# Mixture-of-experts routing of a hybrid decoder trunk: squares summed row by row on TensorE, and the routing stage's steps in another order

## Chip, cores and metric

One core of one Trainium2 chip. The metric is the device time of one execution in microseconds (us), of which the median of several runs is given. A profile is one execution recorded by the hardware profiler; its "span" runs from the first to the last recorded instruction, and times inside it count from the span's start.

## What is computed

Two layers on 512 tokens of width 1024. The first is a gated short convolution with a dense SwiGLU channel mixer, the second is multi-head latent attention with a routed channel mixer: of 8 experts each token uses the best 2. The change lies between the attention's output projection and the first expert. Cut to that part, the reference is:

```python
x = x + mla_mixer(h, ...)                       # ends in  o @ w_o
h = rmsnorm(x, norm_ffn[1])
probs = softmax(h @ router)
vals, idx = lax.top_k(probs, 2)
gates = one_hot(idx) weighted by vals / sum(vals)
for e in range(8):
    out = out + gates[:, e:e+1] * swiglu(h, w_gate[e], w_up[e], w_down[e])
x = x + out
```

All products are wanted at fp32 quality. The kernel splits each operand into a high and a low part (xh and xl, w_hi and w_lo) and adds up two or three products.

## The kernel before, in words

The residual stream lies transposed in `xT`: 8 rows ("fo") of 128 features by 512 tokens. From the attention on, the program's order on each engine is the order in which the code is written out; nothing is reordered by a planner. An engine's queue is worked off in order, so an instruction that waits holds up all that stands behind it on that engine.

The stage of the change runs in these steps.

- Output projection, a loop over 8 rows (line 877). TensorE makes six matmuls of 512 columns (`out_mm`, lines 688 to 690) and, from the third row on, two for the router's logits of the row two before (`logits`, lines 872 and 873; the second needs `xlr`, the low half of that row). VectorE adds the row to `xT` (line 882), makes the low half of the row before (line 888) and one eighth of the first expert weight chunk's low half (line 120). ScalarE makes the high half (885), the squares (891) and one eighth of the chunk's high half (117). GpSimd adds the squares to `acc` (893).
- Token rows. The experts gather whole tokens, so `xT` is transposed back, in 8 blocks of 128 tokens by 512 features. `rows_mm(i)` (line 909) makes four transposes into one PSUM bank. `rows_ev(i)` makes a scaled high half on ScalarE (line 914) and then, out of the same bank and that high half, the low half on VectorE (line 915). `base(i)` (line 921) copies the same bank unscaled to `hs`, mostly on ScalarE, and SyncE sends `hs` to the output.
- Norm and ranking. The sum of squares over features comes from matmuls of one column with `acc` as stationary operand (942). The norm `r3` is a power on GpSimd (line 248, from line 1137). Ranking the 8 logits of a token takes VectorE lines 1139 to 1149 and ends in `sel`. Matmuls with `tri` and `ones_b` count positions into `pc` (1151 to 1153), VectorE turns them into `pos` (1159) and one-hot columns `oh1` (1168). `keep_warm(n)` issues n matmuls whose result is not used (949).
- Picks. Expert 0's tokens are taken by matmuls with `oh1`: `pick(f, 0)` from the high and `pick(f, 1)` from the low half of the token rows, four matmuls each (1189), for 8 rows f. Each picked bank is scaled to `xe` by ScalarE (1200) and VectorE (1201). Then the first expert's matmuls start (1033).
- Expert 0's one-hot list for the gather of its token numbers is made on GpSimd (`select`, 968); GpSimd also issues the four transfers of the token rows to DRAM (1181).

PSUM has 8 banks. Two hold `plt` (later `idle`, which also serves `rows_mm(6)`) and `misc`; six go round in turn among the projection's rows, the transposed rows and the picked rows. Before the change these are, in order: rows_mm 0 to 5 and 7, then picks 0 to 7; each takes the bank of the sixth allocation before it.

Of the kernel before, what the change touches and what calls it, by code (L numbers as in the profile page):

```python
# [11 lines left out]
F32 = mybir.dt.float32  # L12
F32R = mybir.dt.float32r
BF16 = mybir.dt.bfloat16
I32 = mybir.dt.int32
AF = mybir.ActivationFunctionType
# [139 lines left out]
def hybrid_trunk_kernel(ctx, tc, xT_in, pos_in, vecs_in, rope_g, invf_in, ident_in, cst_in, info_in, dslot_in,  # L156
# [713 lines left out]
    def logits(fo):  # L870
        xh, xl = split.pop(fo)
        mm(plt[0:2 * NE, :], rhl[:, fo, :], xh, start=fo == 0, stop=False)
        mm(plt[0:NE, :], rhl[:, fo, 0:NE], xl, start=False, stop=fo == NB - 1)

    ws.pool, ws.ahead, ws.limit, ws.manual = wmoe, 2, len(chunks), True
    pieces = ws.split([256] * 8, True)
    for fo in range(NB):
        ps = ops.tile([P, T], F32, name="ps", tag="ps")
        pairs[3].out_mm(ps, fo)
        if fo >= 2:  # L880
            logits(fo - 2)
        tt(xT[:, fo, :], ps, xT[:, fo, :], ALU.add)
        xh = ot.tile([P, T], F32R, name="xhr", bufs=3)
        xl = ot.tile([P, T], F32R, name="xlr", bufs=3)
        nc.scalar.copy(xh, xT[:, fo, :])
        if fo > 0:
            pxh, pxl = split[fo - 1]
            tt(pxl, xT[:, fo - 1, :], pxh.bitcast(F32), ALU.subtract)
        split[fo] = xh, xl
        sq = acc if fo == 0 else ot.tile([P, T], F32, name="sq", tag="sq")  # L890
        act(sq, xT[:, fo, :], AF.Square)
        if 0 < fo < NB - 1:
            nc.gpsimd.tensor_tensor(acc, acc, sq, ALU.add)
        if fo < NB - 1:
            next(pieces)
    tt(xl, xT[:, NB - 1, :], xh.bitcast(F32), ALU.subtract)
# [7 lines left out]
    def rows_mm(i, ps=None):  # L904
        hf, tb = divmod(i, TB)
        ps = ps or ops.tile([P, T], F32, name="ps", tag="ps")
        hps.append(ps)
        for j in range(4):
            nc.tensor.transpose(ps[:, j * P:(j + 1) * P], xT[:, hf * 4 + j, tb * P:(tb + 1) * P], ident)
# [7 lines left out]
    def base(i, copy):  # L917

        hf, tb = divmod(i, TB)
        hs = bp.tile([P, T], F32, name="hs")  # L920
        copy(hs, hps[i])
        nc.sync.dma_start(out[tb * P:(tb + 1) * P, hf * T:(hf + 1) * T], hs)

    for i in range(4):
        rows_mm(i)
    logits(NB - 2)
    logits(NB - 1)
    rows_mm(4)
    for i in range(2):
        base(i, nc.scalar.copy)  # L930
    lgt = ot.tile([2 * NE, T], F32, name="lgt", bufs=1)
    nc.scalar.copy(lgt, plt[0:2 * NE, :])
    tt(acc, acc, sq, ALU.add)
    for i in range(2, 4):
        base(i, nc.vector.tensor_copy)
    list(pieces)
    for tb in range(TB):
        nc.tensor.transpose(misc[:, tb * 2 * NE:(tb + 1) * 2 * NE], lgt[:, tb * P:(tb + 1) * P],
                            ident[0:2 * NE, 0:2 * NE])
    for tb in range(TB):  # L940
        t_s = slice(tb * P, (tb + 1) * P)
        mm(pss[:, tb:tb + 1], acc[:, t_s], ones[:, 0:1], start=tb == 0, stop=tb == TB - 1)
    rows_mm(5)
    idle = lps.tile([P, T], F32, name="plt")

    def keep_warm(n):

        for _ in range(n):
            mm(idle, ones_b, ones_b[:, None, :].to_broadcast([P, TB, P]), start=True, stop=True)

    keep_warm(6)
    ws.split_hi()
    for i in range(4, 6):
        base(i, nc.scalar.copy)
    octx.close()


# [168 lines left out]
    def ot1(shape, name, dt=F32):  # L1126
        return ot.tile(shape, dt, name=name, tag=name)
# [19 lines left out]
    rank = cpool.tile(sh3, F32, name="rank")  # L1147
    nc.vector.tensor_reduce(rank, cmp, axis=AX.X, op=ALU.add)
    ts(sel_b, rank, 2.0, None, op0=ALU.is_lt)

    mm(pc, tri, sel, start=True, stop=False)
    for tb in range(TB):
        mm(pc[:, tb + 1:, :], ones_b, sel[:, tb:tb + 1, :].to_broadcast([P, TB - tb, NE]), start=False, stop=tb == TB - 1)
    keep_warm(6)
    rows_mm(6, idle)
    mx = ot1([P, TB], "mx4")
    nc.vector.tensor_reduce(mx, lg, axis=AX.X, op=ALU.max)
    pos = cpool.tile(sh3, F32, name="pos")
    stt(pos, pc[:, 0:TB, :], 1.0, sel_b, op0=ALU.add, op1=ALU.mult)
    cnt = cpool.tile([P, NE], F32, name="cnt")  # L1160
    nc.vector.tensor_copy(cnt, pc[:, TB, :])
    ex = [Expert(ws.chunk, e % 2, CAPS[e]) for e in range(NE)]


# [1 line left out]
    oh1 = ot1([P, TB, c0], "oh1", F32R)  # L1166
    for tb in range(TB):
        ts(oh1[:, tb], iota[:, 0:c0], pos[:, tb, 0:1], None, op0=ALU.is_equal)
    ex[0].select(pos[:, :, 0:1])
    xe2 = ep.tile([P, NB, 2, 2, CAP], F32R, name="xe", bufs=1)  # L1170
    xb2 = ep.tile([P, NB, 2, CAP], BF16, name="xb", bufs=1)
    ex[0].hold()
    for i in range(8):
        rows_ev(i)
        if i == 0:
            rows_mm(7)
    for i in (6, 7):
        base(i, nc.scalar.copy)
    for part, op in enumerate((ALU.bypass, ALU.add)):
        for hf in range(2):  # L1180
            nc.gpsimd.dma_start(hrow.rearrange("(t p) d -> p t d", p=P)[:, :, hf * T:(hf + 1) * T],
                                tr[part][hf].bitcast(F32), accum_op=op)
    picked = {}

    def pick(f, part):
        if part == 0:
            picked[f] = ops.tile([P, T], F32, name="ps", tag="ps")[:, 0:c0]
        for tb in range(TB):
            mm(picked[f], tr[part][f // 4][:, tb, (f % 4) * P:(f % 4 + 1) * P], oh1[:, tb],
               start=part == 0 and tb == 0, stop=part == 1 and tb == TB - 1)  # L1190

    pick(0, 0)
    for f in range(NB):
        if f < NB - 1:
            pick(f + 1, 0)
        pick(f, 1)
        pv = picked[f]
        g = col(V_FFN1 + f)
        xe = ex[0].xe
        act(xe[:, f, 0, :], pv, AF.Copy, scale=g)  # L1200
        stt(xe[:, f, 1, :], pv, g, xe[:, f, 0, :].bitcast(F32), op0=ALU.mult, op1=ALU.subtract)
        if f % 4 == 3:
            f4 = slice(f - 3, f + 1)
            nc.scalar.copy(ex[0].xb[:, f4, :], xe[:, f4, 0, :].bitcast(F32))
# [114 lines left out]
    for e in range(NE):  # L1319
        x, nxt, prv = ex[e], ex[e + 1] if e + 1 < NE else None, ex[e - 1] if e else None  # L1320
        for c in range(24):
            storing = prv and prv.nh == 2 and 0 < c < 5
            loading = nxt and NF <= c < NF + LOADS
            if storing:
                prv.store_mm(c - 1)
            if loading:
                nxt.load_mm(c - NF)
            if c < NF:
                x.hidden_mm(c)
                if c > 2 and c % 2:  # L1330
                    x.hidden_split(c // 2 - 1)
                if c and c % 2 == 0:
                    x.hidden_gate()
                x.hidden_add(c)
            else:
                x.down_mm(c - NF)
                if c == NF:
                    x.hidden_gate()
                if c == NF + 1:
                    x.hidden_split(NF // 2 - 1)  # L1340
                if c % 4 == 3:
                    (x.down_add if nxt else last_store)((c - NF) // 4)
            if storing:
                prv.store_ev(c - 1)
            if loading:
                nxt.load_ev(c - NF)
            if prv and c == (2 if prv.nh == 2 else 0):
                prv.store(0)

            if prv and c == 13 and prv.nh == 2:  # L1350
                prv.store(1)
            if not nxt and c == 11:
                last_base()
            if ws.n_split <= last_k:
                ws.split_hi()
            if ws.n_lo <= last_k:
                ws.split_lo()
            while ws.n_raw <= min(ws.n_split - 1 + len(ws.ring), last_k):
                list(ws.load())
            if e == 1 and c == 10:  # L1360
                extra_rows()
            if e == 0:
                if c == 0:
                    rank_experts()
                if c == 1:
                    x.find(0)
                    ranked(posn, pos)
                    ranked_weights()
                if c in (2, 3):
                    nxt.select(posn[:, :, 0:1], (2 * c - 4, 2 * c - 3))  # L1370
                if c == 3:
                    ranked_gates()
                if c == 4:
                    xctx.close()
                    xtctx.close()
                    late.append(right(ctx, "late"))
                    ws.grow(late[0], 2)
            if e + 2 < NE and NF <= c < NF + TB:
                ex[e + 2].select(posn[:, :, e + 2 - NS:e + 3 - NS], (c - NF,))
            if nxt and c == 6:  # L1380
                nxt.find(e + 1)
                nxt.gather()
# [205 lines left out]
```

## Time and profile before

| | us |
|---|---|
| median of 3 runs | 1408.69 (1407.62 to 1410.09) |
| the profiled execution | 1409.13 |
| its span | 1407.4 |
| stage of the change, projection of the first row to the first expert matmul | 748.3 to 786.3 |

TensorE is busy for 98% of the span, VectorE for 71%, ScalarE for 58%, GpSimd for 20%. In the profile PE is TensorE's matmuls and PEld its weight loads, which overlap; DVE is VectorE, ACT ScalarE, POOL GpSimd, SP SyncE. A row of a timeline gives start, duration, engine, line, operation, output and input, the number of instructions merged into it, and in brackets the idle time before it with what ended that.

### The profile page before, as it was taken

Reading aid. Unit: us, or ns where it says so; the run is one execution under the profiler, and the core shown is the slowest. Engines: PE = TensorE matmul, PEld = TensorE weight load, DVE = VectorE, ACT = ScalarE, POOL = GpSimd, SP = SyncE. Lnnn points to the kernel's source line nnn. Section 1 sums busy time; section 2 is a strip of 40 time slices with the busy share of each in tenths; the row PEclk is TensorE's granted clock in tenths of the full one; section 3 lists DMA queues with packets and bytes.
Section 4 is the critical chain, followed back from the end, with each engine's and each line's share of the span. In section 5 each row is a group of like instructions: output and inputs, shape, how many; then the busy total and the mean of one; then the engine's idle time right before and its main releaser. Section 6 shows DMA issues by size and latency. Waiting matters only on the chain. (4 is left out here: it accounts for less than half of the span.)

```text
span 1407.4 us, 23788 instructions
## 1 busy us (share of the span) xinstructions
PE 1375.7 (98%) x9543; PEld 1197.0 (85%) x9544; DVE 993.4 (71%) x1263; ACT 815.2 (58%) x1210; POOL 286.1 (20%) x206
## 2 busy tenths in 40 slices
PE   9999999999999999999998999999999999999996
PEld 6888888888888887878876899999999999979794
DVE  7754565442344444587788897898889899999895
ACT  6222332222222233677645787878888788988893
POOL 0000000000000000143302432342614343453231
PEclk9999999999999999999999999999999999999998
DMA  6332222322223222101203999998999999999993
GB/s 223 112 115 91 90 90 94 116 90 90 90 93 117 91 90 92 64 31 63 82 10 149 310 358 373 308 331 300 347 329 334 360 341 368 321 400 370 384 364 104
DMA packets 49390, 284.40 MB, mean 202 GB/s; under 512 B 9320, under 2 KB 11112, under 8 KB 17272
## 3 DMA queue, kind: packets, MB, share of 16 engines
q1 hardware_dynamic: 41688, 269.82, 52.7%
q0 software_dynamic: 7584, 12.98, 3.9%
q8 instruction: 77, 1.26, 0.4%
q14 instruction: 41, 0.34, 0.1%
HBM read 271.39 MB, written 11.37 MB: 201 GB/s over the span
## 5 line engine op out<-in xcount | busy, mean ns | idle before, releaser
L97 DVE TENSOR_TENSOR w_lo<-w_raw,w_hi 128x2048 bf16<-128x2048 f32 (+1 forms) x239 | 556.9, 2330 | 53.9 <-ACT w_hi L88 53.6
L88 ACT CAST w_hi<-w_raw 128x2048 fp32r<-128x2048 f32 x239 | 456.6, 1910 | 221.5 <-PE ps L256 158.8
L1033 PE MATMUL gu<-xe,w_hi 128*128 128x304 f32 (+6 forms) x2048 | 288.9, 293 | 0.0
L1033 PEld LDWEIGHTS gu<-xe,w_hi 128*128 128x128 f32 x2048 | 264.1, 189 | 0.4
L255 PE MATMUL ps<-xh,w_hi 128*128 128x512 f32 x592 | 232.4, 393 | 2.2 <-ACT xh L290 1.3
L256 PE MATMUL ps<-xl,w_hi 128*128 128x512 f32 x592 | 231.0, 390 | 0.3 <-DVE xl L291 0.3
L257 PE MATMUL ps<-xh,w_lo 128*128 128x512 f32 x592 | 231.1, 390 | 0.0
L1047 POOL TENSOR_TENSOR sg<-sg,p 128x304 f32<-128x304 f32 (+6 forms) x64 | 88.0, 1374 | 304.6 <-ACT sg L1046 300.6
L1033 PE MATMUL gu<-xb,w_lo 128*128 128x152 bf16 (+6 forms) x2048 | 143.4, 223 | 3.9 <-DVE w_lo L97 3.9
L255 PEld LDWEIGHTS ps<-xh,w_hi 128*128 128x128 f32 x592 | 111.5, 188 | 26.8 <-ACT xh L290 1.8
L256 PEld LDWEIGHTS ps<-xl,w_hi 128*128 128x128 f32 x592 | 111.6, 188 | 24.1 <-DVE xl L291 0.8
L1033 PEld LDWEIGHTS <-w_lo 128*128 128x128 bf16 x2048 | 120.6, 98 | 12.8 <-DVE w_lo L97 5.8
L257 PEld LDWEIGHTS ps<-xh,w_lo 128*128 128x128 f32 x592 | 111.5, 188 | 23.3
L248 POOL TENSOR_TENSOR rs<-m,mhalf 128x4 f32<-128x4 f32 x3 | 3.1, 1020 | 590.8 <-DVE m L505 555.9
L1077 PE MATMUL gu<-ae,w_hi 128*128 128x304 f32 (+3 forms) x640 | 97.4, 302 | 0.0
L257 PE MATMUL ps<-ah,w_lo 128*128 128x512 f32 x240 | 94.7, 394 | 0.0
L255 PE MATMUL ps<-ah,w_hi 128*128 128x512 f32 x240 | 94.6, 394 | 0.0
L256 PE MATMUL ps<-al,w_hi 128*128 128x512 f32 x240 | 94.6, 394 | 0.0
L1077 PEld LDWEIGHTS gu<-ae,w_hi 128*128 128x128 f32 x640 | 87.1, 189 | 0.0
L1041 DVE TENSOR_TENSOR p<-gu,p 128x304 f32<-128x304 f32 (+6 forms) x128 | 55.7, 435 | 23.7 <-ACT p L1040 22.5
L1040 ACT COPY p<-gu 128x304 f32<-128x304 f32 (+6 forms) x128 | 49.3, 385 | 38.7 <-PE gu L1033 38.0
L968 POOL TENSOR_SCALAR oh<-rest,posn 128x152 bf16<-128x152 f32 (+6 forms) x28 | 60.1, 2159 | 1.3 <-DVE posn L1258 1.3
(334 smaller groups left out, 1878.7 us busy)
## 6 DMA issues: line engine op xcount, KB each, us to landing
w_raw<-w_moe SPq DMA_DIRECT2D x192, 1024.0 KB, 8.5
w_raw<-w_a SPq DMA_DIRECT2D x50, 1024.0 KB, 4.8
w_raw<-w_hp SPq DMA_DIRECT2D x4, 1088.0 KB, 5.1
w_raw<-w_o SPq DMA_DIRECT2D x4, 1024.0 KB, 4.7
xT<-xT_in SPq DMA_DIRECT2D x8, 256.0 KB, 5.0
out<-hs SPq DMA_DIRECT2D x8, 256.0 KB, 4.1
hrow<-xh POOLq DMA_DIRECT2D x2, 1024.0 KB, 5.9
hrow<-xl POOLq DMA_DIRECT2D x2, 1024.0 KB, 23.6
```

Of the source, the lines that this page charges most:

```text
L88: self.nc.scalar.copy(hi[:, :w], self.raw[k][:, :w])
L97: self.nc.vector.tensor_tensor(lo[:, :w], self.raw.pop(k)[:, :w], self.hi[k][:, :w].bitcast(F32), ALU.subtract)
L248: nc.gpsimd.tensor_tensor(out_t, m, h, ALU.pow)
L255: mm(ps, wh, xh[:, kc, :], start=kc == 0, stop=False)
L256: mm(ps, wh, xl[:, kc, :], start=False, stop=False)
L257: mm(ps, wl, xh[:, kc, :], start=False, stop=kc == n - 1)
L968: nc.gpsimd.tensor_scalar(s.oh[:, tb, 0:s.cap], iota[:, 0:s.cap], p[:, tb], None, op0=ALU.is_equal)
L1033: mm(s.ps[:, i, 0:n], w[:, b:b + P], x[:, kc], start=w is hi and kc == 0, stop=w is lo and kc == NB - 1)
L1040: nc.scalar.copy(p2, s.ps[:, :, s.cap:2 * s.cap])
L1041: tt(p2, s.ps[:, :, 0:s.cap], p2, ALU.add)
L1047: nc.gpsimd.tensor_tensor(s.sg, s.sg, s.p2[:, :, 1], ALU.mult)
L1077: mm(s.dp[q // 2][:, q % 2, 0:n], w[:, b:b + P], x[:, 4 * kq + j], start=w is hi and kq + j == 0, stop=w is lo and kq + j == 6)
```

## The change

It makes these edits.

1. Squares. GpSimd no longer adds them up. `square_sums(fo)` makes four matmuls of one column per row, with the row's squares as stationary operand, accumulated over all rows in `pss`. Rows 0 to 5 are summed inside the loop, two rows late; rows 6 and 7 behind their logits. VectorE's last addition of squares and the four matmuls on `acc` go.
2. Order on TensorE after the loop: logits and squares of rows 6 and 7, then the transposes of the logits, then `rows_mm(4)`, 6 warming matmuls; `rows_mm(5)` moves among the picks.
3. `base(2)` and `base(3)` go from VectorE to ScalarE. `base(4)` and `base(5)` move from ahead of the norm to behind `rows_ev` of the same block.
4. The high half of the second weight chunk (`ws.split_hi`, 128x2048 on ScalarE) moves from ahead of the token rows to behind `base(7)`, which is ahead of the picks' evictions.
5. `rows_ev(0)` stands ahead of the counting, `rows_ev(1)` to `rows_ev(4)` behind `oh1`, `rows_ev(5)` to `rows_ev(7)` each followed by its `base`. The second warming has 4 matmuls, not 6. `cnt` and `mx` move behind.
6. `select` of expert 0 moves on GpSimd from ahead of the four transfers to between the second and the third, and `find(0)` from the expert's chunk 1 to chunk 2.
7. The picks of high halves run two rows ahead of the low ones, not one.

```diff
+    sqs = {}
+
+    def square_sums(fo):
+        sq = sqs.pop(fo)
+        for tb in range(TB):
+            mm(pss[:, tb:tb + 1], sq[:, tb * P:(tb + 1) * P], ones[:, 0:1],
+               start=fo == 0 and tb == 0, stop=fo == NB - 1 and tb == TB - 1)
+
     for fo in range(NB):
         ps = ops.tile([P, T], F32, name="ps", tag="ps")
         pairs[3].out_mm(ps, fo)
         if fo >= 2:
+            square_sums(fo - 2)
             logits(fo - 2)
...
-        sq = acc if fo == 0 else ot.tile([P, T], F32, name="sq", tag="sq")
-        act(sq, xT[:, fo, :], AF.Square)
-        if 0 < fo < NB - 1:
-            nc.gpsimd.tensor_tensor(acc, acc, sq, ALU.add)
+        sqs[fo] = acc if fo % 3 == 2 else ot.tile([P, T], F32, name="sq", tag="sq")
+        act(sqs[fo], xT[:, fo, :], AF.Square)
...
-    logits(NB - 2)
-    logits(NB - 1)
-    rows_mm(4)
+    for fo in (NB - 2, NB - 1):
+        logits(fo)
+        square_sums(fo)
...
-    tt(acc, acc, sq, ALU.add)
-    for i in range(2, 4):
-        base(i, nc.vector.tensor_copy)
...
-    for tb in range(TB):
-        t_s = slice(tb * P, (tb + 1) * P)
-        mm(pss[:, tb:tb + 1], acc[:, t_s], ones[:, 0:1], start=tb == 0, stop=tb == TB - 1)
-    rows_mm(5)
+    for i in range(2, 4):
+        base(i, nc.scalar.copy)
+    rows_mm(4)
...
     keep_warm(6)
-    ws.split_hi()
-    for i in range(4, 6):
-        base(i, nc.scalar.copy)
...
     ts(sel_b, rank, 2.0, None, op0=ALU.is_lt)
+    rows_ev(0)
...
-    keep_warm(6)
-    rows_mm(6, idle)
+    keep_warm(4)
...
-    ex[0].select(pos[:, :, 0:1])
...
-    for i in range(8):
+    for i in range(1, 5):
         rows_ev(i)
-        if i == 0:
-            rows_mm(7)
-    for i in (6, 7):
-        base(i, nc.scalar.copy)
...
     pick(0, 0)
+    rows_mm(5)
+    base(4, nc.scalar.copy)
+    pick(1, 0)
+    rows_mm(6, idle)
+    rows_mm(7)
+    for i in range(5, 8):
+        rows_ev(i)
+        base(i, nc.scalar.copy)
+    ws.split_hi()
...
+    for part, op in enumerate((ALU.bypass, ALU.add)):
+        for hf in range(2):
+            nc.gpsimd.dma_start(hrow..., tr[part][hf].bitcast(F32), accum_op=op)
+        if part == 0:
+            ex[0].select(pos[:, :, 0:1])
     for f in range(NB):
-        if f < NB - 1:
-            pick(f + 1, 0)
+        if f < NB - 2:
+            pick(f + 2, 0)
         pick(f, 1)
...
+                if c == 2:
+                    x.find(0)
                 if c == 1:
-                    x.find(0)
```

## Rows read from the trace of the kernel before

**Rows 1.** The page: span, then busy time, share of the span, instructions.
```profile
span 1407.4 us, 23788 instructions
...
PE 1375.7 (98%) x9543; PEld 1197.0 (85%) x9544; DVE 993.4 (71%) x1263; ACT 815.2 (58%) x1210; POOL 286.1 (20%) x206
```

**Rows 2.** Busy time by stretch: projection loop, ranking, counting, the experts.
```profile
core 0: us, PE busy (x) PEld busy (x) DVE busy (x) ACT busy (x) POOL busy (x), PEclk, DMA share, GB/s
752.50:766.50 14.00, 11.19 (x46) 6.84 (x45) 14.00 (x18) 8.94 (x20) 7.30 (x6) 1.00 0.54 229
...
770.90:775.50 4.60, 4.58 (x22) 2.88 (x23) 3.05 (x10) 4.60 (x7) 1.02 (x1) 0.65 0.86 315
775.50:778.60 3.10, 2.81 (x21) 1.63 (x19) 2.70 (x9) 2.55 (x6) 2.40 (x4) 0.96 1.05 332
...
900.00:1000.00 100.00, 99.79 (x989) 97.16 (x989) 85.57 (x92) 80.22 (x100) 37.56 (x21) 1.00 0.92 322
```

**Rows 3.** Timeline of PE: projection loop and what follows it.
```profile
751.83 0.39 PE L688 MATMUL ps<-xh,w_hi 128*128 128x512 f32 x1
...
753.67 0.40 PE L688 MATMUL ps<-xh,w_hi 128*128 128x512 f32 x1
...
766.54 1.91 PE L909 MATMUL ps<-ident,xT 128*128 128x128 f32 x16
768.21 0.47 PE L872 MATMUL plt<-xhr,rhl 128*16 128x512 f32 x1
...
770.92 0.42 PE L938 MATMUL misc<-ident,lgt 16*128 16x16 f32 x4 [0.39 <-ACT lgt L932]
...
775.53 0.24 PE L1151 MATMUL misc<-sel,tri 128*128 128x40 bf16 x1
```

**Rows 4.** Timeline of PEld: square sums, transposes and warming at half clock, picks.
```profile
771.27 0.97 PEld L942 LDWEIGHTS misc<-ones,acc 128*128 128x128 f32 x8
772.08 0.71 PEld L909 LDWEIGHTS ps<-ident,xT 128*128 128x128 f32 x4
772.76 0.36 PEld L949 LDWEIGHTS <-ones_b 128*128 128x128 bf16 x2
...
783.13 0.52 PEld L1189 LDWEIGHTS ps<-oh,xh 128*128 128x128 f32 x4 [0.26 <-ACT hs L921]
...
786.25 2.40 PEld L1033 LDWEIGHTS gu<-xe,w_hi 128*128 128x128 f32 x16
```

**Rows 5.** Timeline of DVE: low half beside POOL and alone, positions, token rows.
```profile
754.18 1.66 DVE L888 TENSOR_TENSOR xlr<-xT,xhr 128x512 fp32r<-128x512 f32 x1
...
757.79 0.68 DVE L888 TENSOR_TENSOR xlr<-xT,xhr 128x512 fp32r<-128x512 f32 x1
...
775.90 0.19 DVE L1159 SCALAR_TENSOR_TENSOR pos<-misc,sel 128x32 f32<-128x32 f32 x1 [1.57 <-PE misc L1153]
...
777.11 4.03 DVE L915 SCALAR_TENSOR_TENSOR xl<-ps,r,xh 128x512 fp32r<-128x512 f32 x6
781.06 0.74 DVE L915 SCALAR_TENSOR_TENSOR xl<-plt,r,xh 128x512 fp32r<-128x512 f32 x1
781.72 0.74 DVE L915 SCALAR_TENSOR_TENSOR xl<-ps,r,xh 128x512 fp32r<-128x512 f32 x1
```

**Rows 6.** Timeline of ACT: weight chunk, token rows, their copies, the picks' evictions.
```profile
771.08 1.89 ACT L88 CAST w_hi<-w_raw 128x2048 fp32r<-128x2048 f32 x1
772.88 1.05 ACT L921 COPY hs<-ps 128x512 f32<-128x512 f32 x2
...
778.60 0.69 ACT L914 ACTIVATE xh<-ps,r 128x512 fp32r<-128x512 f32 x1 [0.26 <-PE ps L909]
781.83 0.59 ACT L921 COPY hs<-plt 128x512 f32<-128x512 f32 x1 [2.55 <-DVE xl L915]
782.49 0.59 ACT L921 COPY hs<-ps 128x512 f32<-128x512 f32 x1
782.98 1.23 ACT L1200 ACTIVATE xe<-ps,vec 128x152 fp32r<-128x152 f32 x4
```

More of the change, by code (lines that the diff above doesn't have):

```diff
@@ L1153, in hybrid_trunk_kernel @@
         mm(pc[:, tb + 1:, :], ones_b, sel[:, tb:tb + 1, :].to_broadcast([P, TB - tb, NE]), start=False, stop=tb == TB - 1)
-    keep_warm(6)
-    rows_mm(6, idle)
-    mx = ot1([P, TB], "mx4")
-    nc.vector.tensor_reduce(mx, lg, axis=AX.X, op=ALU.max)
+    keep_warm(4)
     pos = cpool.tile(sh3, F32, name="pos")
     stt(pos, pc[:, 0:TB, :], 1.0, sel_b, op0=ALU.add, op1=ALU.mult)
-    cnt = cpool.tile([P, NE], F32, name="cnt")
-    nc.vector.tensor_copy(cnt, pc[:, TB, :])
     ex = [Expert(ws.chunk, e % 2, CAPS[e]) for e in range(NE)]
@@ L1168, in hybrid_trunk_kernel @@
         ts(oh1[:, tb], iota[:, 0:c0], pos[:, tb, 0:1], None, op0=ALU.is_equal)
-    ex[0].select(pos[:, :, 0:1])
-    xe2 = ep.tile([P, NB, 2, 2, CAP], F32R, name="xe", bufs=1)
-    xb2 = ep.tile([P, NB, 2, CAP], BF16, name="xb", bufs=1)
-    ex[0].hold()
-    for i in range(8):
-        rows_ev(i)
-        if i == 0:
-            rows_mm(7)
-    for i in (6, 7):
-        base(i, nc.scalar.copy)
[L1179 to L1182, printed above, removed]
+    for i in range(1, 5):
+        rows_ev(i)
     picked = {}
@@ L1192, in hybrid_trunk_kernel @@
     pick(0, 0)
+    rows_mm(5)
[7 more added lines that the diff above has]
+    ws.split_hi()
+    cnt = cpool.tile([P, NE], F32, name="cnt")
+    nc.vector.tensor_copy(cnt, pc[:, TB, :])
+    mx = ot1([P, TB], "mx4")
+    nc.vector.tensor_reduce(mx, lg, axis=AX.X, op=ALU.max)
+    xe2 = ep.tile([P, NB, 2, 2, CAP], F32R, name="xe", bufs=1)
+    xb2 = ep.tile([P, NB, 2, CAP], BF16, name="xb", bufs=1)
+    ex[0].hold()
+    for part, op in enumerate((ALU.bypass, ALU.add)):
+        for hf in range(2):
+            nc.gpsimd.dma_start(hrow.rearrange("(t p) d -> p t d", p=P)[:, :, hf * T:(hf + 1) * T],
+                                tr[part][hf].bitcast(F32), accum_op=op)
+        if part == 0:
+            ex[0].select(pos[:, :, 0:1])
     for f in range(NB):
-        if f < NB - 1:
-            pick(f + 1, 0)
+        if f < NB - 2:
+            pick(f + 2, 0)
         pick(f, 1)
```

## Prediction

> **What bounds the kernel now.** I read the page first: TensorE is busy for 98% of the span, every other engine for 71% or less [rows 1]. A share over the whole span doesn't say what a stage is worth, so the next view was busy time by stretch. In the experts, from 786 us to the end nearly, PE is busy for 99.79 of 100 us at full clock [rows 2]. Nothing there can make up for a late start: what the stage before hands over late is late at the end. So the number to forecast is the start of the first expert matmul, 786.25 us by its weight load [rows 4].
>
> The stage before it has three parts, and their limits differ. In the projection loop VectorE is busy for 14.00 of 14.00 us while TensorE has 11.19 [rows 2]: TensorE waits for `xlr`. The reader sees why in the timeline of VectorE: the same subtraction takes 0.68 us alone and 1.66 us while GpSimd adds squares [rows 5]. In ranking and counting the granted clock of TensorE is 0.65 on average, that is a mix of 2.4 and 1.2 GHz [rows 2]. In the last part VectorE makes the eight low halves one behind the other, 777.11 to 782.46 [rows 5], and TensorE's picks follow, each as soon as a PSUM bank and the rows are there; the only wait in it was 0.26 us for a copy to `hs` [rows 4].
>
> **Part 1, the loop.** One row with logits is eight matmuls, 751.83 to 753.67: 1.84 us [rows 3]. Six such rows make 11.04 us; from 751.83 to the first token-row transpose at 766.54 it took 14.71 [rows 3]. The 3.67 us between are the wait for VectorE. With GpSimd's additions gone, VectorE has per row two operations of 0.68 us [rows 5] and a smaller one, below a row of TensorE, so I count that wait as gone. What is late next is TensorE itself: `square_sums` is eight passes per row. The same eight passes on `acc` ran from 771.27 to 772.08, 0.81 us [rows 4]; by the price of a transpose, 1.67 us for 16 from 766.54 to 768.21 [rows 3], they would be 0.84. A pass has one column only, and its weight load sets the pace, so they don't hide beside the matmuls. The loop becomes 6 x (1.84 + 0.81) = 15.9 us: it ends at 767.73, 1.2 us later than before. Bounds: if half of each sum hides behind 512-column matmuls, 1.2 us earlier than before; if the loads run at 0.97 us per row (the whole span of the eight loads [rows 4]), 2.2 us later. I take 0.81, the operation's own row.
>
> **Part 2, from the loop to the positions.** TensorE then has 16 transposes (1.67), two logits pairs (0.46 each, a quarter of 1.84), two square sums (0.81 each): 767.73 + 4.21 = 771.94. The logits' copy on ScalarE fits beside the last sum. The four small transposes take 0.35 (770.92 to 771.27 [rows 3, 4]), `rows_mm(4)` 0.5 to 0.7, six warming matmuls at half clock 2.77 (772.76 to 775.53 [rows 3, 4]): the counting starts at about 775.5 to 775.8, as before. The norm, a little ahead of where it was, and `rows_ev(0)` lie beside the warming. So `pos` comes at 775.8, before at 775.90 [rows 5]. Between `pos` and the first low half lay 1.21 us [rows 5], half of it `oh1` beside GpSimd's `select`; without that I take 0.7. Then VectorE makes rows 1 to 4 at 0.66 us each (781.06 to 781.72): 776.5 + 3 x 0.66 + 0.74 = 779.2 for the end of row 4, bounds 778.5 and 780.5. Up to here the change costs nothing: the later loop is paid by the square sums that no longer stand behind it and by row 0 done early.
>
> **Part 3, the step that decides.** ScalarE's `base(i)` and VectorE's `rows_ev(i)` read the same PSUM bank. In the trace `base(6)` sat idle for 2.55 us and started at 781.83; VectorE's row 6 ended at 781.06 + 0.74 = 781.80. `base(7)` started at 782.49; VectorE's row 7 ended at 782.46 [rows 5, 6]. Nothing in the data asks for it (both only read), so I read the two coincidences as a wait of the copy for the other reader of its bank.
>
> The Trainium skill, PSUM — Partial Sum Buffer, section on bank collisions, says that two engines may not be in one bank and quadrant at once, reads against reads included, and that software has to order them. By that rule the wait comes back wherever a copy follows a row's low half; without it the sum is that of the first rival below. The two coincidences agree with the rule.
>
> Before, the two copies stood behind all eight rows. Now ScalarE's queue is base(4), row 5, base(5), row 6, base(6), row 7, base(7), `split_hi`, then the first eviction `xe`. base(4) waits for VectorE's row 4; queued behind it is ScalarE's half of row 5, without which VectorE can't make row 5, for which base(5) waits. The engines take turns, and one turn is 0.48 (copy to next start, half of the 0.96 between 772.88 and the row behind) + 0.69 (row) + 0.74 (VectorE) + 2 x 0.03 (the gaps above) = 1.97 us [rows 5, 6]. base(4) starts at 779.2, base(7) three turns later at 785.15, `split_hi` at 785.6. That takes 1.80 (771.08 to 772.88 [rows 6]), so the first eviction runs at 787.45, and with some 0.4 us on each of ScalarE and VectorE (an estimate: four evictions take ScalarE 1.23 [rows 6], overlapping) its bank is free at 788.25.
>
> Who waits for that: six banks go round. Rows 0 to 4, pick 0, row 5, pick 1, row 7, pick 2 and pick 3 come first in this order, so pick 4 needs the bank of pick 0. TensorE reaches `pick(4, 0)` after four half picks, three rows' transposes and two more half picks at the latest, near 781, and stands until 788.25. Behind it are ten of the sixteen half picks. Seven took 783.13 to 786.25, 0.446 each [rows 4]; ten take 4.45. The first expert matmul starts at 792.7 instead of 786.25: 6.45 us later. Running the high picks two rows ahead hides nothing of it, as it is the bank and not the low half that is missing; and `split_hi`, which ScalarE did before while it had to wait for the norm anyway, now costs its whole 1.80 us.
>
> **Clock.** TensorE stands for 7 us. In the trace the clock was at 2.4 GHz through the loop and fell in the ranking stretch, which holds short transposes, one-column passes and waits: 0.65 over 4.6 us and 0.96 over 3.1 us [rows 2] are 3.2 + 0.25 = 3.5 us at 1.2 GHz. I expect the same behind the stand. Four transposes took 0.68 us at 1.2 GHz (772.08 to 772.76 [rows 4]) against 0.42 (a quarter of 1.67 [rows 3]) at full clock. A half pick of 0.446 would be some 0.67 to 0.72, an estimate from that ratio; in 3.5 us five are done where nearly eight would be: 1.1 us lost. Bounds: 0, and 2.5 if the low stretch is twice as long or reaches into the expert.
>
> The Trainium skill, TensorE: Matmul & The Clock Gate, part 1, puts it as "the default state is throttled, and activity releases the throttle". It speaks against any order that leaves TensorE standing; by it the 1.1 us is owed, without it the sum is 1.1 us less.
>
> **Edits with one answer.** `select` later on GpSimd: its four operations (2.40 us [rows 2]) now stand behind two transfers that wait for row 7's high half, at 784.3; its list is first read in the third chunk of expert 0, over 64 matmuls behind the first, at 0.1 us each (989 in 100 us [rows 2]) 6 us: 799. The `hs` transfers on SyncE, with weight loads queued behind them, leave 2.7 us later (base(7) at 785.15, not 782.49), the experts that need the weights 7.5. `base(2)`, `base(3)` on ScalarE fit while it waits for the norm; uncovered they would cost 0.96 [rows 6]. `cnt` and `mx` lie in VectorE's idle turns, and are of the size of `pos`, 0.19 [rows 5]. I count nothing.
>
> **The sum.** 6.45 + 1.1 = 7.55 us. Profiled execution 1409.13 (span 1407.4 and 1.73 around it) + 7.55 = 1416.7; that execution lies 0.44 above the median 1408.69, so against the median 1416.2.
>
> **Rivals.** First, the copies don't wait for VectorE's read (the 2.55 us had another cause). Then ScalarE runs through: base(4), three rows and three copies from about 777.3, held only by the transposes, ending near 781.6; `split_hi` to 783.4, bank of pick 0 free at 784.2, ten half picks to 788.6: 2.4 us late, perhaps 0.6 for the clock, 1411.4. For it: no data dependence. Against it: two starts within 0.03 us of the other reader's end.
>
> Second, not slower: neither the copies nor the banks hold the picks, if evictions come in time (say the ScalarE order on the chip is not the written one, or banks are taken as they fall free). Before, the first pick had to wait for the bank of row 1, free at 777.11 + 0.66 + 0.74 = 778.5 [rows 5]; now it starts when `oh1` is there, near 777, carries three more blocks of transposes (3 x 0.42) and saves the 0.26 wait: 0.5 us earlier, 1408.2. It decides if pick 0's bank is free by 781. Against it: the bank order seen in the 0.26 us wait, where pick 5 took row 7's bank behind its copy [rows 4, 6].
>
> Third, slower still: the one-column passes, a third of a loop row, let the clock fall in the loop already or keep it low into the expert. 6 rows of 1.84 us at 1.2 GHz for part of the loop and a longer low stretch cost 2 to 4 us more: 1419. Against it: the loop before had waits of a quarter of its time (3.67 of 14.71) at clock 1.00 [rows 2, 3].
>
> **How the numbers follow.** Forecast 0.72, its own range 1414.0 to 1418.3 (stand 1 us shorter or longer, clock 0 to 2.5). First rival 0.11, second 0.09, third 0.08. To leave out no more than 2 in 10 the range takes in the first rival and not the second: 1410.8 to 1418.8. About 0.2% (2.8 us) is what a measurement can tell from no change: slower 0.83, same 0.13 (the second rival and a part of the first), faster 0.04.
>
> **What the profile after would show.** Right: on ScalarE, `hs` copies of rows 4 to 7 each idle behind VectorE's L915 equivalent, some 2 us apart; the 128x2048 cast between the last of them and the first `xe`; TensorE idle for about 7 us in the picks, released by VectorE's or ScalarE's `xe`; clock near 0.5 behind it; no GpSimd work in the loop, VectorE's subtractions all near 0.68, the loop about 1 us longer. Wrong: copies back to back, or no stand in the picks, or a loop that is shorter.

## The result and the profile after

The changed kernel takes 1416.33 us (median; 1415.17 to 1420.12), the kernel before 1408.69; the ratio is 1.0053, with a 95% interval of 1.0038 to 1.0067. The forecast was 1416.2. The profiled execution took 1415.87 us, 6.74 more than that of before. The total came out as forecast, but two of the terms behind it were wrong by some 2 us each and a third was missing. They cancelled, so it is luck that the total came this close.

The page of the kernel after, to be read beside [rows 1], shows this: 6.7 us more span, and TensorE's share is unchanged.

```profile
span 1414.1 us, 23890 instructions
...
PE 1383.4 (98%) x9595; PEld 1208.5 (85%) x9598; DVE 985.1 (70%) x1260; ACT 816.8 (58%) x1212; POOL 278.8 (20%) x200
```

The busy time by stretch, kernel after, with the columns of [rows 2], shows where the limits moved.

```profile
752.50:766.50 14.00, 14.00 (x86) 11.75 (x85) 9.20 (x18) 8.95 (x20) 0.10 (x1) 1.00 0.56 233
770.90:775.50 4.60, 4.39 (x33) 2.76 (x31) 2.97 (x10) 3.48 (x7) 1.01 (x1) 1.00 0.59 171
...
783.00:786.00 3.00, 1.68 (x7) 1.48 (x7) 0.92 (x4) 2.14 (x4) 1.45 (x2) 0.50 0.34 128
786.00:792.00 6.00, 5.49 (x26) 5.28 (x26) 1.60 (x5) 3.73 (x8) 4.37 (x6) 0.50 1.03 327
792.00:796.00 4.00, 4.00 (x19) 4.00 (x19) 2.73 (x4) 3.04 (x5) 0.14 (x1) 0.50 1.02 208
796.00:797.00 1.00, 1.00 (x8) 0.91 (x8) 0.89 (x3) 0.57 (x2) 0.00 (x0) 0.90 1.13 209
```

Line by line against [rows 2]: in the projection loop VectorE fell from 14.00 busy to 9.20 of 14 and TensorE rose from 11.19 to 14.00. In the ranking stretch the granted clock rose from 0.65 to 1.00. In the picks TensorE stands (1.68 busy of 3.00), and the clock, at 0.50, stays there while TensorE is busy for all of 792 to 796.

The next two fences are ScalarE's and VectorE's timelines after (start, duration, engine, line, operation, operands, number, and in brackets the idle time and its end), to be read beside [rows 5, 6].

```profile
779.05 0.58 ACT L928 COPY hs<-ps 128x512 f32<-128x512 f32 x1 [2.20 <-DVE xl L922]
...
781.04 0.58 ACT L928 COPY hs<-ps 128x512 f32<-128x512 f32 x1 [0.82 <-DVE xl L922]
...
783.04 0.58 ACT L928 COPY hs<-plt 128x512 f32<-128x512 f32 x1 [0.82 <-DVE xl L922]
...
785.03 0.58 ACT L928 COPY hs<-ps 128x512 f32<-128x512 f32 x1 [0.82 <-DVE xl L922]
785.51 1.90 ACT L88 CAST w_hi<-w_raw 128x2048 fp32r<-128x2048 f32 x1
787.31 1.22 ACT L1206 ACTIVATE xe<-ps,vec 128x152 fp32r<-128x152 f32 x4
```

```profile
775.24 0.18 DVE L1157 SCALAR_TENSOR_TENSOR pos<-misc,sel 128x32 f32<-128x32 f32 x1
...
776.29 2.72 DVE L922 SCALAR_TENSOR_TENSOR xl<-ps,r,xh 128x512 fp32r<-128x512 f32 x4
780.26 0.75 DVE L922 SCALAR_TENSOR_TENSOR xl<-ps,r,xh 128x512 fp32r<-128x512 f32 x1 [1.24 <-ACT xh L921]
```

Each `hs` copy of blocks 4 to 7 is released by VectorE's low half of the same block, 1.99 us apart, and VectorE in its turn idles for ScalarE's high half of the next block (1.24 us for block 5, which ends at 781.01; its copy starts at 781.04). Then comes the weight cast, and only then the first eviction `xe`. Last, TensorE's timeline after, to be read beside [rows 3, 4].

```profile
753.20 0.95 PE L882 MATMUL misc<-ones,sq 128*128 128x1 f32 x8
754.01 0.40 PE L872 MATMUL plt<-xhr,rhl 128*16 128x512 f32 x1
...
767.64 1.91 PE L916 MATMUL ps<-ident,xT 128*128 128x128 f32 x16
...
781.68 0.93 PE L1173 MATMUL ps<-oh,xh 128*128 128x152 f32 x3 [0.87 <-ACT hs L928]
784.26 0.50 PE L1173 MATMUL ps<-oh,xh 128*128 128x152 f32 x1 [1.66 <-ACT xh L921]
...
785.67 1.13 PE L1173 MATMUL ps<-oh,xh 128*128 128x152 f32 x4
...
788.17 1.14 PE L1173 MATMUL ps<-oh,xh 128*128 128x152 f32 x4 [0.51 <-DVE xe L1207]
...
790.81 2.76 PE L1173 MATMUL ps<-oh,xl 128*128 128x152 f32 x12
793.37 3.73 PE L1033 MATMUL gu<-xe,w_hi 128*128 128x304 f32 x16
796.94 1.23 PE L1033 MATMUL gu<-xb,w_lo 128*128 128x152 bf16 x16
797.96 2.21 PE L1033 MATMUL gu<-xe,w_hi 128*128 128x304 f32 x14
```

The first expert matmul starts at 793.37, before at 786.32. Its first chunk (16 matmuls with `w_hi`, 16 with `w_lo`) ends at 797.96, 4.60 us later; before, the chunk took 3.44.

For all kernels below one table cuts TensorE's timeline in the same places: "loop" is from the first matmul of the output projection to the first token-row transpose, "stage" from there to the first expert matmul, then expert 0's first chunk and its chunks 2 to 14. "Against before" is the sum of the four less that of before (87.72); below it is called the ledger. These are single executions; the ratio in the last column is of medians.

| kernel | loop | stage | chunk 1 | 2 to 14 | against before | ratio to before [95%] |
|---|---|---|---|---|---|---|
| before | 18.25 | 19.78 | 3.44 | 46.25 | | |
| after | 19.31 | 25.73 | 4.60 | 44.82 | +6.7 | 1.0053 [1.0038, 1.0067] |
| r1_copies_first | 19.31 | 18.28 | 3.46 | 46.39 | -0.3 | 1.0017 [1.0006, 1.0028] |
| r2_split_early | 19.31 | 24.94 | 5.50 | 44.84 | +6.9 | 1.0064 [1.0045, 1.0083] |
| r3_both | 19.31 | 17.47 | 3.46 | 46.90 | -0.6 | 1.0015 [1.0002, 1.0027] |
| r4_fill | 19.31 | 23.28 | 3.46 | 46.38 | +4.7 | 1.0062 [1.0041, 1.0083] |
| r5_squares_only | 19.30 | 18.02 | 3.45 | 46.24 | -0.7 | 0.9998 [0.9985, 1.001] |
| r6_turns_only | 18.22 | 27.47 | 4.13 | 45.60 | +7.7 | 1.0052 [1.0032, 1.0071] |
| r7_both_select | 19.31 | 17.62 | 3.45 | 46.91 | -0.4 | 1.0011 [0.9996, 1.0026] |
| r8_pairs | 19.45 | 16.81 | 3.44 | 46.91 | -1.1 | 0.9998 [0.9987, 1.001] |
| r9_after_again | 19.30 | 25.73 | 4.41 | 45.46 | +7.2 | 1.0047 [1.0031, 1.0063] |
| r10_fill_again | 19.30 | 23.28 | 3.46 | 46.39 | +4.7 | 1.0041 [1.0025, 1.0057] |
| r11_pairs_late | 16.22 | 17.62 | 3.46 | 50.03 | -0.4 | 0.9979 [0.9968, 0.999] |

### The profile page after: what moved, and what is told of

Read it like the earlier page. It is cut to its first block, busy times and chain, and to the rows that moved or that the text cites. A ratio compares the mean times of both kernels' runs of the same rounds, so it can differ in the third digit from the quotient of the medians.

```text
span 1414.1 us, 23890 instructions
## 1 busy us (share of the span) xinstructions
PE 1383.4 (98%) x9595; PEld 1208.5 (85%) x9598; DVE 985.1 (70%) x1260; ACT 816.8 (58%) x1212; POOL 278.8 (20%) x200
```

## Experiments

The theory: the loss comes from ScalarE's copies and VectorE's low halves taking turns on PSUM banks (edit 5 with the end of edit 3), lengthened by the cast behind them (edit 4) and by the clock; the squares cost nothing. The rivals: something else holds the copies (the `hs` buffers, SyncE); the clock alone sets the picks; the one-column passes hold the clock down.

**r1_copies_first.** The kernel after, with each copy of blocks 4 to 7 ahead of the low half of its block, nothing else.

```diff
     for i in range(1, 5):
+        if i == 4:
+            base(4, nc.scalar.copy)
         rows_ev(i)
...
     rows_mm(5)
-    base(4, nc.scalar.copy)
...
     for i in range(5, 8):
-        rows_ev(i)
         base(i, nc.scalar.copy)
+        rows_ev(i)
```

> The kernel after, with each copy base(4) to base(7) put ahead of the row step of its own block instead of behind it; nothing else moves. Theory (ScalarE's copy waits for VectorE's read of the same bank, and the two engines take turns): no copy idles behind VectorE any more, ScalarE does copy and row back to back (about 1.15 us a block), VectorE's eight low halves end near 781 instead of 785.0, the 128x2048 cast ends near 783, pick 0 is evicted near 783.3 and the first expert matmul starts near 786 instead of 793.2, at full clock. Time: about 7 us off the kernel after, 1409.5 (1408 to 1411.5). Rival (the copies wait for something of their own, the hs buffers or the transfers on SyncE): the copies still idle about 0.8 us each, and the time stays within 2 us of the kernel after, 1414.5 to 1417.

ScalarE's timeline in this kernel:

```profile
777.38 0.60 ACT L928 COPY hs<-ps 128x512 f32<-128x512 f32 x1
777.84 0.73 ACT L921 ACTIVATE xh<-ps,r 128x512 fp32r<-128x512 f32 x1
778.57 0.59 ACT L928 COPY hs<-ps 128x512 f32<-128x512 f32 x1
...
781.73 1.94 ACT L88 CAST w_hi<-w_raw 128x2048 fp32r<-128x2048 f32 x1
```

No copy idles, the cast starts at 781.73 (785.51 after), the stage takes 18.28 us instead of 25.73, and the first chunk is back at 3.46. The same copies go into the same `hs` buffers and onto the same queue, so the rival that `hs` or SyncE holds them falls. The turns hold most of the loss: the ratio falls from 1.0053 to 1.0017 (1.0006 to 1.0028), and why it is not 1.0 was not settled.

**r2_split_early.** The kernel after, with the cast moved back ahead of the logits' copy.

```diff
     for i in range(2):
         base(i, nc.scalar.copy)
+    ws.split_hi()
...
-    ws.split_hi()
     cnt = cpool.tile([P, NE], F32, name="cnt")
```

> The kernel after, with the 128x2048 cast of the second weight chunk put behind base(1), where ScalarE stood idle for 1.85 us waiting for the logits; the turn-taking of copies and rows stays. Theory (the cast is one link of the chain that holds pick 6): the first eviction of a pick runs at 785.5 instead of 787.3, and pick 6 starts 1.8 us earlier; at half clock TensorE may then be the limit, so 1.0 to 2.0 us off the kernel after: 1414.8 (1414 to 1415.6). Rival (the half clock alone sets the picks, the bank's wait of 0.5 us is all there is to win): at most 0.7 us, 1415.6 to 1416.5.

First ScalarE's, then TensorE's timeline in this kernel:

```profile
784.20 0.59 ACT L928 COPY hs<-ps 128x512 f32<-128x512 f32 x1 [0.82 <-DVE xl L922]
784.68 0.95 ACT L1206 ACTIVATE xe<-ps,vec 128x152 fp32r<-128x152 f32 x3
```

```profile
788.33 1.05 PE L1174 MATMUL ps<-oh,xh 128*128 128x152 f32 x4
789.18 2.76 PE L1174 MATMUL ps<-oh,xl 128*128 128x152 f32 x12
791.74 4.34 PE L1034 MATMUL gu<-xe,w_hi 128*128 128x304 f32 x16
795.89 1.56 PE L1034 MATMUL gu<-xb,w_lo 128*128 128x152 bf16 x16
```

The eviction comes behind the last copy at once, and no pick waits for it any more. Yet the picks still run at half clock (1.05 us a row of four), the stage is only 0.8 shorter, and the half clock then reaches further into the expert: the first chunk takes 5.50, not 4.60. The expected gain was missed (1417.18 us, where 1414.8 was expected); the answer is nearer to the rival, in which the half clock sets the picks. Once the turns have made TensorE stand, the clock paces the picks, and the place of the cast decides little.

**r3_both.** Both edits of r1 and r2.

> Both edits of the two runs before in one kernel: copies ahead of their rows, the cast in ScalarE's idle time before the logits. Theory: pick 0 is evicted near 781.5, TensorE runs through the picks from about 775.9 with 16 half picks (7.1 us) and three blocks of transposes (1.4 us), the first expert matmul starts near 784.5 to 785, before the 786.25 of the kernel before, at full clock. Time 1407.5 (1406 to 1409). Rival (what the loop lost to the square sums, 1.1 us, and the half clock stay): 1410 to 1412.

Without the stand the cast is worth 0.81 us (stage 17.47 against 18.28). The stage came out nearly as expected, the time did not: 1409.5 us (ratio 1.0015), where a small gain was expected. Behind the four columns of the table, the end of expert 0 and the first matmul of expert 1 took 36.63 us, 34.81 before. In the list of TensorE's waits from 836 to 878 us (who waited, for what; us in total, times, longest) expert 1's start stands on its gathered rows:

```profile
PE tp L1011 <- DMA xr<-hrow,ids: 1.6, 1, 1.6
```

**r7_both_select.** r3 with expert 0's `select` back ahead of the four transfers on GpSimd, to see whether the late list holds that gather.

```diff
+    ex[0].select(pos[:, :, 0:1])
     for i in range(1, 5):
...
-        if part == 0:
-            ex[0].select(pos[:, :, 0:1])
```

> Copies first and cast early, as in r3, and in addition expert 0's one-hot list made on GpSimd ahead of the four transfers again, as in the kernel before. Theory (in r3 the gather for expert 1 came 1.6 us late, since the transfers of the token rows stood behind that list): no wait for gathered rows at the start of expert 1, the rest as in r3; loop 19.31, from there to the first expert matmul 17.5, in all 1.2 us less than the kernel before: 1407 (1405.5 to 1409). Rival (the late gather is the transfers' own time): the wait of 1.6 us stays and the time is that of r3, 1409.5.

TensorE's waits from 745 to 1400 us in this kernel:

```profile
PE tp L1011 <- DMA xr<-hrow,ids: 6.9, 3, 3.7
```

The wait at expert 1 is still there (1.1 us of the 6.9, after 1.6 in r3), and the ratio is 1.0011. The list is not what holds most of it; the theory of `select` falls, and the transfers of the token rows are left as the likely cause. The trace supports that but doesn't settle it: GpSimd idles for 7.7 us ahead of the fourth transfer, 1.5 in the kernel before, and ahead of its gather for expert 1 it idles for 5.6 us more, 3.2 before.

**r4_fill and r10_fill_again.** The kernel after, with 26 matmuls of 384 columns whose result is not used, put where TensorE stands.

```diff
+    def fill(n):
+        for _ in range(n):
+            mm(misc[:, P:], ones_b, ones_b[:, None, :].to_broadcast([P, 3, P]), start=True, stop=True)
...
+            if (f, part, tb) == (4, 0, 3):
+                fill(9)
...
         if f < NB - 2:
+            fill({2: 5, 3: 3, 4: 9}.get(f, 0))
             pick(f + 2, 0)
```

> The kernel after with 26 matmuls of 384 columns put where TensorE stands in the picks (5 ahead of pick 4, 9 ahead of its last matmul, 3 ahead of pick 5, 9 ahead of pick 6); their result is not used and no wait is changed; the copy of the counts moves up behind the positions. Theory (half of the loss is the clock: half picks at 0.86 us instead of 0.446 behind the stand, and 1.15 us in the first expert chunk): granted clock stays 1.00, pick 6 still waits for the eviction until 788.2, the six half picks behind it take 2.7 us, the first expert matmul starts at 790.9 instead of 793.2; 3.5 us in all, of which the experts give back less afterwards: 1413.5 (1412.5 to 1414.5). Rival (the slow half picks come of memory traffic, transfers and GpSimd at the same time, not of the clock): half picks stay at 0.86 us and the time does not move, 1415.5 to 1417.

Busy time and clock from 780 to 790 us, then TensorE's timeline:

```profile
780.00:790.00 10.00, 9.53 (x66) 6.77 (x66) 3.91 (x9) 7.09 (x13) 4.67 (x6) 1.00 0.75 261
```

```profile
788.09 0.67 PE L1181 MATMUL ps<-oh,xh 128*128 128x152 f32 x4
...
790.83 2.59 PE L1033 MATMUL gu<-xe,w_hi 128*128 128x304 f32 x16
```

At full clock the stage takes 23.28: this separates the two terms. Without the half clock the first expert matmul comes 19.31 + 23.28 - (18.25 + 19.78) = 4.56 us later than before (the longer loop and the waits in the picks, less what ranking saves); the half clock adds 25.73 - 23.28 = 2.45 in the picks and 4.60 - 3.46 = 1.14 in the first chunk. In the experts part of it comes back (chunks 2 to 14 take 46.38 with the fill, 44.82 without). The rival of memory traffic falls with the four matmuls of a half pick, 0.67 us instead of 1.14. The time itself did not follow: 1416.52 us in r4, where 1413.5 was expected, so kernel after and fill ran once more side by side.

> The changed kernel as it is, beside the next two on one chip, so that they can be set against it. Every theory: 7 to 8 us above the kernel before, 1416; the loop 19.31 us, the first expert matmul 25.7 us behind it.

> The kernel of r4 (26 matmuls without use where TensorE stands) with more executions, against r9. Theory (the half clock costs 3.5 us up to the first expert chunk, and the experts give back 1.4 us of it in waits for weights that a late start spares): 2.0 us below r9 (1.0 to 3.0). Rival (what the clock costs is given back in full later on): within 0.7 us of r9.

The medians are 1416.7 us (after) and 1415.04 (fill): 1.7 less, with overlapping intervals. The trace shows 3.4 us less up to the end of chunk 1 (2.45 and 0.95) and 0.93 given back behind it. Taken together, the ratios of the fill (1.0062 and 1.0041) and of the kernel after (1.0053 and 1.0047) don't differ clearly: what the clock costs is shown up to chunk 14, in the traces, and not in the whole time.

**r5_squares_only.** The kernel before, with edit 1 alone (GpSimd's additions out, four one-column matmuls per row in).

> The kernel before with the squares alone moved to TensorE, row by row as in the change (rows 6 and 7 behind the transposes of row block 4); all else as before. Theory (the loop becomes TensorE's, 0.81 us a row against 3.67 us of waits that go): the loop ends 1.1 us later, as it did in five profiles of kernels with this edit; VectorE's subtractions all near 0.68 us; the stage behind the loop is shorter by what GpSimd and VectorE no longer add there, 0 to 0.7 us; the first expert matmul 0.5 to 1.2 us later. Time 0 to 1.5 us above the kernel before: 1408.8. Rival (the loss of the whole change comes with this edit, one-column passes holding the clock down): 4 us or more above, 1412 and up, with the granted clock below 1 in the loop or the picks.

Busy time in the ranking stretch of this kernel:

```profile
770.00:774.00 4.00, 4.00 (x35) 3.43 (x33) 2.06 (x5) 2.95 (x4) 0.00 (x0) 1.00 0.71 262
```

The loop is 1.05 us longer, the stage 1.76 shorter, the clock 1.00; the ratio is 0.9998. The rival that the passes hold the clock down falls, and with r6, which has none of them in the loop and the same low clock in the picks, once more.

**r6_turns_only.** The kernel before, with the copies of blocks 4 to 7 each behind its low half and the cast behind them; squares, picks and `select` as before.

```diff
     keep_warm(6)
-    ws.split_hi()
-    for i in range(4, 6):
-        base(i, nc.scalar.copy)
...
-    for i in (6, 7):
-        base(i, nc.scalar.copy)
+        if i > 3:
+            base(i, nc.scalar.copy)
+    ws.split_hi()
```

> The kernel before with one part of the change alone: base(4) to base(7) each directly behind the row step of its own block, and the 128x2048 cast behind base(7). Theory (turns of copy and row, then the cast, are the loss): four copies idle about 0.8 us each behind VectorE's low half, 1.99 us a turn, base(7) near 786.4, cast to 788.7, first expert matmul 6 to 8 us later than 786.3, picks and first expert chunk at half clock for part of it. Time 6 to 8 us above the kernel before: 1415. Rival (the turns only hurt together with the picks two ahead or the later loop): 0 to 3 us above, 1408 to 1411.

ScalarE's timeline, then the busy time by stretch:

```profile
778.90 0.59 ACT L921 COPY hs<-ps 128x512 f32<-128x512 f32 x1 [3.63 <-DVE xl L915]
...
780.89 0.59 ACT L921 COPY hs<-ps 128x512 f32<-128x512 f32 x1 [0.82 <-DVE xl L915]
...
785.36 1.90 ACT L88 CAST w_hi<-w_raw 128x2048 fp32r<-128x2048 f32 x1
```

```profile
770.00:772.00 2.00, 2.00 (x12) 1.77 (x12) 1.44 (x6) 0.00 (x0) 0.79 (x1) 0.57 1.02 350
784.00:794.00 10.00, 9.32 (x40) 8.91 (x41) 4.08 (x10) 6.71 (x14) 3.45 (x3) 0.50 0.94 260
```

The turns and the low clock are those of the kernel after, and so is the ratio, 1.0052. Through chunk 14 the two halves, -0.7 (r5) and +7.7 (r6), add up to +7.0, where the whole change has +6.7. The picks two rows ahead, the later `select` and the other moves are left with about nothing, within what two executions of the changed kernel differ by (+6.7 and +7.2 in r9).

**r8_pairs.** Built on r7: VectorE adds the squares of two rows, TensorE sums four pairs, not eight rows, and the cast is cut in four pieces in the loop.

```diff
+    def add_pair(p):
+        a, b = sqs[2 * p], sqs[2 * p + 1]
+        tt(a, a, b, ALU.add)
...
-            square_sums(fo - 2)
+            if fo % 2:
+                square_sums((fo - 3) // 2)
...
+            c = slice((fo - 2) * 512, (fo - 1) * 512)
+            nc.scalar.copy(ws.hi[k1][:, c], ws.raw[k1][:, c])
```

> r7 with two edits more: VectorE, idle for a third of the loop, adds the squares of two rows, so that TensorE sums four tiles instead of eight; and the second chunk's high half is cast in four pieces inside the loop, where ScalarE idles, not ahead of the logits. Theory (a row's sum costs TensorE 0.81 us on the path, in the loop and behind it): loop 19.31 - 3 x 0.81 = 16.9, from there to the first expert matmul 17.5 - 0.8 = 16.7; together 33.6 against 38.0 in the kernel before, 4.4 us less, of which the experts take back 0.5 in waits for weights: 1404.0 (1402.5 to 1406). Rival (VectorE's additions put its old limit back, or the pieces make ScalarE late): loop 18 or more, time 1406 to 1408.5.

TensorE's timeline in the loop:

```profile
754.49 1.02 PE L889 MATMUL misc<-ones,acc 128*128 128x1 f32 x8 [0.73 <-DVE acc L884]
```

The passes are halved, but the loop is no shorter (19.45): TensorE waits for VectorE's addition, here 0.73 us, 1.7 in all. The stage did gain (16.81). The time was 1408.78 us, where 1404.0 was expected: missed, and the wait showed what to change.

**r11_pairs_late.** r8 with each pair summed one row later.

```diff
-            if fo % 2:
-                square_sums((fo - 3) // 2)
+            if fo > 2 and fo % 2 == 0:
+                square_sums(fo // 2 - 2)
...
-    square_sums(NB // 2 - 1)
+        square_sums(fo - NB // 2)
```

> r8 with each pair's sum on TensorE one row later in the loop, so that it does not wait for VectorE's addition: pairs 0 and 1 in rows 4 and 6, pairs 2 and 3 behind the logits of rows 6 and 7. Theory: no wait of TensorE for the additions, loop 16.3 to 16.6 us (two sums, not three, and no waits), from there to the first expert matmul 17.4 to 17.7; in all 34.0 against 38.0 in the kernel before. In the experts 0.7 us more of waits for weights and 1 to 2 us for the gathered rows of expert 1, which are bound by the transfers: 2 us below the kernel before, 1406.5 (1405 to 1408). Rival (the transfers, at nine tenths or more of their time from 772 us on, take back all of it): 1408 to 1409.5, with the waits for gathered rows larger by what the stage gained.

TensorE's timeline at the loop's end and in the experts, and its waits from 790 to 836 us:

```profile
764.56 1.91 PE L934 MATMUL ps<-ident,xT 128*128 128x128 f32 x16
...
826.36 1.99 PE L1051 MATMUL gu<-xb,w_lo 128*128 128x152 bf16 x16 [1.89 <-DVE w_lo L97]
828.08 3.37 PE L1051 MATMUL gu<-xe,w_hi 128*128 128x304 f32 x16
```

```profile
PE gu L1051 <- DVE w_lo L97: 3.1, 2, 1.9
```

This one beats both kernels: 1406.61 us (ratio 0.9979, 0.9968 to 0.999), 2.5 us below the before that ran beside it. Loop and stage are 4.2 us shorter than before (33.84 against 38.03), but the experts, starting earlier, wait 3.1 us for low halves of weights (1.1 before in the same stretch), and chunks 2 to 14 take 3.8 back. The waits are 2.0 of it. Most of the rest is the clock, which fell again behind the longest of them: 0.66 from 825 to 830 us, where 16 matmuls took 1.99 and 3.37 us that take 1.23 and 2.48 in the chunks beside them. So the total came as expected (1406.5), but the experts took it back by other waits than the expected ones for gathered rows. In the profiled execution that leaves 0.4; the medians say more. Where the rest of the 2.5 lies was not settled, as single executions of one kernel differ by some 6 us (1403.4 to 1409.86 here). The same holds for r1, 2.4 us above before by its ratio though its ledger is at -0.3.

## Why the prediction held, point by point

- **The loop: right.** VectorE's wait is gone, the eight passes take 754.01 - 753.20 = 0.81 us, and the loop ends 1.06 later (19.31 against 18.25); 1.2 was forecast.
- **To the positions: right in time, wrong in one cause.** I took the six warming matmuls at half clock, as before [rows 2]; the clock was 1.00 there, 0.65 before. `pos` came at 775.24 instead of 775.8, and rows 1 to 4 ended at 776.29 + 2.72 = 779.01; 779.2 was forecast.
- **The turns: right.** Forecast were 779.2, 1.97 a turn, 785.15 and 785.6 for the cast, 787.45 for the eviction; measured 779.05, 1.99, 785.03, 785.51 and 787.31. The Trainium skill, PSUM — Partial Sum Buffer, section on bank collisions, wants two readers of a bank ordered by software; the 0.82 us of idle time, released by VectorE's `xl`, and its absence in r1 agree with that.
- **The cast: right in place, wrong in price.** I put its whole 1.80 us on the path. With the cast moved away (r2) the stage is 0.79 us shorter and the first chunk 0.90 longer, and the ledger stays at +6.9: behind the stand the half clock paced the picks, not the eviction.
- **The banks: wrong.** I let pick 4 wait for the bank of pick 0, six allocations before, from 781 to 788.25 in one stand. It started at 781.68, released by the copy `base(5)` (781.04 + 0.58 = 781.62), and its last matmul waited for row 7's high half until 784.26: the longest wait of all was for data that the turns made late, not for a bank. Pick 5 started at 785.67, behind `base(7)` (785.03 + 0.58 = 785.61), and only pick 6 waited for an eviction, at 788.17. So the banks of rows 5 and 7 went to picks 4 and 5: handed out by which has its last use first in the program, as these starts read (the allocation itself is not in the trace), not by turn. In the kernel before both rules give the same banks, by the order of its code, so the 0.26 us wait that I took as proof could not tell them apart. The stand of 7 us fell into four shorter waits with picks between, 3.2 us in TensorE's list of waits, and the first expert matmul came 4.56 us late without the half clock (r4), where the step had 6.45.
- **The clock: right in kind, wrong in size.** Forecast 1.1 us, bounds 0 to 2.5; measured 2.45 in the picks and 1.14 in the expert, 3.6. Both factors were too low (and with my own, five half picks lose 1.1 to 1.4 us; I took the low end). I took the 3.5 us at half clock of before [rows 2] as the pattern; it lasted from about 782.5 to 796.1, with TensorE busy for 5.49 of 6.00 and 4.00 of 4.00 us. And I took a half pick at half clock at 0.67 to 0.72; three of them took 790.81 to 793.37, 0.85 each. That price came from four transposes, 772.08 to 772.76, read as wholly at half clock, but the clock fell in their midst, as the stretches of the kernel before show behind this list. "Reaches into the expert" stood among the bounds, and their end was too low. The Trainium skill, TensorE: Matmul & The Clock Gate, part 1, says that activity releases the throttle. The traces agree in direction, as filled stands kept 1.00 (r4); the 10 us at 0.50 with TensorE busy for 9.49 of them (786 to 796) don't come out of that sentence, and there the measurement decides.
- **"Nothing there can make up for a late start": wrong.** Chunks 2 to 14 took 44.82 us, not 46.25. The list of waits of before has 1.1 us for low halves of weights from 790 to 836 (second fence behind this list), that of after none: a start 8 us later finds the weights ready. The gain isn't steady: the same kernel got 0.8 back in r9, and r4, 4.6 us late, nothing. In r11, starting early, the same stretch costs 3.8 more. I had read 99.79 of 100 us busy from 900 to 1000, which says nothing of the 50 us behind the first expert matmul.
- **Edits counted at nothing: right.** r5 and r6 together leave no more than 0.3 us for them in the ledger.

Two views of the kernel before, for the clock and for the weights. First, busy time and clock while the four transposes ran:

```profile
771.50:772.00 0.50, 0.50 (x7) 0.50 (x6) 0.50 (x2) 0.50 (x1) 0.00 (x0) 1.00 1.04 385
772.00:772.50 0.50, 0.50 (x5) 0.50 (x6) 0.26 (x3) 0.50 (x1) 0.00 (x0) 0.81 0.98 348
772.50:773.00 0.50, 0.50 (x5) 0.44 (x4) 0.47 (x3) 0.50 (x2) 0.40 (x1) 0.50 1.11 402
```

Then TensorE's waits from 790 to 836 us:

```profile
PE gu L1033 <- DVE w_lo L97: 1.1, 2, 0.9
```

The sum: 6.45 + 1.1 = 7.55 was forecast, and 4.56 + 3.6 - 1.4 = 6.7 came, in the profiled executions and up to the end of chunk 14. The medians differ by 7.6. So the mechanism (the turns, the stand they cause, the clock behind it) was right, and the closeness of the sum was luck. The first rival (copies that don't wait) falls with the 0.82 us, the third (passes that slow the clock) with r5. The second was nearer with the banks (not by turn), but its 0.5 us gain fell with the turns: the banks that picks 4 and 5 took came free only behind the copies.

## What to carry to other kernels

Before putting a copy behind another engine's read of the same PSUM bank, write out both queues: if the copy also stands ahead of work that this engine needs, the two take turns, and four copies of 0.58 us became 1.99 us each. Put the copy first, as in r1. Price a stand of TensorE with the clock that follows it, and check in the stage behind whether an earlier start would only meet the next late input.

## What the runs showed of the hardware beyond what was expected

- In the kernel after the clock fell at about 782.5, behind a wait of 0.87 us and three matmuls. It stayed at 0.50 from 783 to 786 (TensorE busy for 1.68 of 3.00 us) and for 10 us more with TensorE busy for 95% (9.49 of 10.00, 786 to 796); in r6 it was 0.50 for all of 784 to 794 (9.32 of 10.00). In the kernel before the fall in the ranking stretch lasted some 3.5 us, worked out from [rows 2].
- One-column passes, a third of TensorE's time in a row of the loop, left the clock at 1.00 in the loop. In the ranking stretch it fell in the two kernels without them in the loop (0.65 before, 0.57 in r6) and stayed at 1.00 after and in r5. What tells these apart was not tried.
